# A 180-degree rotation on one core: the second group's turn in four pieces of 2048 columns instead of six with a split last copy

## The chip, the core and the metric

The kernel runs on one core of one Trainium2 chip. The metric is the device time of one execution in microseconds (us). Before the change it is 121.99 us, the median of three runs (121.90 to 122.02 us).

## What is computed

```python
def setup_inputs():
    batch, c, h, w = 32, 3, 256, 256
    return {"x": np.random.randn(batch, c, h, w).astype(np.float32)}

def reference(x):
    return np.rot90(x, k=2, axes=(-2, -1)).astype(np.float32)
```

Each of the 32 x 3 = 96 images of 256 x 256 float32 values is turned by 180 degrees. Seen as one row of 65,536 values, an image is simply reversed. Input and output are 25.17 MB each.

## The kernel before

The 96 rows are cut into three groups of 32 rows. A row of a group is cut into four quarters of E = 16,384 values, and each quarter lies on a partition of its own, so that a group fills a tile of 128 partitions x 64 KiB. The tiles are A, Bt and Ct for groups 0, 1 and 2. All three fit in on-chip memory at the same time, and a tile is turned in place.

To reverse a row one has to reverse the order of its quarters and reverse each quarter in itself. The order of the quarters is handled by a transfer with a reversed index: for A and Ct by the store (`o4[g][:, ::-1, :]`, line 57), for Bt by the load (line 71). The reversal within a quarter is done by the vector engine.

`turn(t, pieces, parts)` (line 75) walks over the first half of the 16,384 columns in `pieces` steps, and for each calls `swap` (line 59), which exchanges a block of w columns at the left with its mirror block at the right. A swap is three copies through the scratch tile T (128 x 2048): the right block reversed into T, the left block reversed into the right one, T into the left one. If `parts` is over 1, the third copy of the last swap of a turn is cut into that many copies. All copies are recorded in the helper `copy` (line 49), in the order of the program.

All transfers are issued from the sync engine's queue (SP), in this order: load A (line 54), load Bt (line 71), load Ct in two parts of 15,872 and 512 columns (lines 72 and 73), store Bt (line 83), store A (line 57), store Ct (line 57). The queue issues the store of Bt when the last copy of Bt's turn is done; the store of A comes behind it in the queue. The vector engine turns A, then Bt, then Ct. Every turn needs its whole load, and every store its whole turn. The profile puts the copies on line 49, whatever the tile, so the tile's name tells the groups apart.

Of the kernel before, what the change touches and what calls it, by code (L numbers as in the profile page):

```python
# [2 lines left out]

os.environ.setdefault("NEURON_RT_ULTRASERVER_MODE", "4")

# [4 lines left out]


@with_exitstack
def kernel(
    ctx: ExitStack,
    tc: tile.TileContext,
    x: bass.AP,
    out: bass.AP,
):
    nc = tc.nc  # L20
    P = 128

    B, C, H, W = x.shape
    L = H * W
    G = 32
    E = L // 4
    J = E // 8

    x4 = x.rearrange("b c h w -> (b c) (h w)").rearrange(
        "(g n) (s e) -> g (n s) e", n=G, s=4)  # L30
    o4 = out.rearrange("b c h w -> (b c) (h w)").rearrange(
        "(g n) (s e) -> g n s e", n=G, s=4)

    xr = x.rearrange("b c h w -> (b c) (h w)").rearrange(
        "(g n) (s e) -> g n s e", n=G, s=4)
    of = out.rearrange("b c h w -> (b c) (h w)").rearrange(
        "(g n) (s e) -> g (n s) e", n=G, s=4)

    pool = ctx.enter_context(tc.tile_pool(name="slots", bufs=1))
    A = pool.tile([P, E], x.dtype, tag="A")  # L40
    Bt = pool.tile([P, E], x.dtype, tag="B")
    Ct = pool.tile([P, E], x.dtype, tag="C")
    T = pool.tile([P, J], x.dtype, tag="T")

    def back(t, lo, hi):
        return t[:, hi - 1:(lo - 1 if lo else None):-1]

    def copy(dst, src):
        c = nc.vector.tensor_copy(out=dst, in_=src)  # L49
        tc.keep_in_program_order(c)  # L50
        return c

    def load(t, g):
        return nc.sync.dma_start(out=t[:, :], in_=x4[g])  # L54

    def store(t, g):
        return nc.sync.dma_start(out=o4[g][:, ::-1, :], in_=t[:, :])

    def swap(t, lo, w, parts=1):
        hi = E - lo - w  # L60
        copy(T[:, 0:w], back(t, hi, hi + w))
        copy(t[:, hi:hi + w], back(t, lo, lo + w))
        step = -(-w // parts)
        for a in range(0, w, step):
            b = min(w, a + step)
            copy(t[:, lo + a:lo + b], T[:, a:b])

    half = E // 2

    load(A, 0)  # L70
    nc.sync.dma_start(out=Bt[:, :], in_=xr[1][:, ::-1, :])
    nc.sync.dma_start(out=Ct[:, 0:E - 512], in_=x4[2][:, 0:E - 512])
    nc.sync.dma_start(out=Ct[:, E - 512:E], in_=x4[2][:, E - 512:E])

    def turn(t, pieces, parts=1):
        step = -(-half // pieces)
        for lo in range(0, half, step):
            w = min(step, half - lo)
            swap(t, lo, w, parts if lo + w == half else 1)

    turn(A, 4)
    turn(Bt, 6, 2)
    nc.sync.dma_start(out=of[1], in_=Bt[:, :])
    store(A, 0)
    turn(Ct, 4)
    store(Ct, 2)


# [1 line left out]
_INS = ['x']  # L90
_OUTS = [((32, 3, 256, 256), 'float32')]


# [23 lines left out]
```

## Time and profile before

One profiled execution took 121.83 us; its span, from the first instruction to the last, is 120.0 us.

| | |
|---|---|
| median of three runs | 121.99 us |
| profiled execution, time / span | 121.83 / 120.0 us |
| vector engine (DVE) busy | 45.2 us, 43 copies |
| data moved | 25.17 MB read, 25.17 MB written |
| load A landed, turn of A starts | 22.5 us |
| load Bt landed, turn of Bt starts | 41.9 us |
| store of Bt issued | 58.28 us |
| store of A issued | 58.67 us |
| turn of Ct starts | 61.43 us |
| store of Ct issued | 76.55 us |

DVE is the vector engine; SPq is the queue instruction with which the sync engine issues a transfer. "COPY T<-A 128x2048" is a copy from tile A to tile T, of 128 partitions by 2048 columns. The share beside a DMA queue is the time that its packets took, as a share of the span of 16 DMA engines. In a view of a stretch of time, a packet is booked in the slice in which it starts; a packet of these transfers is a whole partition's row (64 KiB) and lasts over 2 us. "Us to landing" is the time from the issue of a transfer to the arrival of its last data.

### The profile page before, as it was taken

The page shows a single profiled execution, that of the slowest core. Times are in us where ns is not written, and L with a number is a line of the kernel's source. Part 1 is how long each engine was busy: PE and PEld are TensorE (multiplying, and loading weights), DVE is VectorE, ACT ScalarE, POOL GpSimd, SP SyncE. Part 2 cuts the span into 40 slices and gives each one's busy share as a digit, 9 for nine tenths or more (in the row PEclk, how much of TensorE's full clock was granted, in tenths as well). Part 3 has the DMA queues.
Part 4 walks back from the last instruction along what each step waited for, and adds up shares of the span by engine and source line. Part 5 has one row for each costly group of instructions (what it writes and reads, how often), then busy time and mean ns, then how long its engine had stood idle before and what let it go on. Part 6 is the DMA issues. An engine that isn't in the chain of part 4 may idle for free.

```text
span 120.0 us, 99 instructions
## 1 busy us (share of the span) xinstructions
DVE 45.2 (38%) x43; POOL 0.2 (0%) x4
## 2 busy tenths in 40 slices
DVE  0000000499995099999359999400000000000000
POOL 0000000000000000000000000000000000000000
DMA  9888988898889878977899889988898889888990
GB/s 349 349 349 371 677 349 349 349 699 349 349 349 677 360 338 360 656 338 338 350 534 590 349 349 415 633 349 349 371 677 349 349 349 699 349 349 349 655 393 0
DMA packets 1008, 50.33 MB, mean 419 GB/s; under 512 B 112, under 2 KB 112, under 8 KB 240
## 3 DMA queue, kind: packets, MB, share of 16 engines
q1 hardware_dynamic: 1008, 50.33, 97.4%
HBM read 25.17 MB, written 25.17 MB: 419 GB/s over the span
## 4 chain that ended last, share of the span: by engine, by line
DMA 34%; DVE 26%; another core or an unknown queue 3%; issue 1%; SPq 0%; DVEq 0%
DMA Bt<-in_x_dram 34%; DVE Bt L49 9%; DVE T L49 9%; DVE Ct L49 8%; SPq L54 0%; DVEq L49 0%
## 5 line engine op out<-in xcount | busy, mean ns | idle before, releaser
L49 DVE COPY T<-A 128x2048 f32<-128x2048 f32 x4 | 4.9, 1226 | 22.6 <-DMA A<-in_x_dram 22.5
L49 DVE COPY T<-Bt 128x1366 f32<-128x1366 f32 (+1 forms) x6 | 5.2, 873 | 4.5 <-DMA Bt<-in_x_dram 4.3
L49 DVE COPY T<-Ct 128x2048 f32<-128x2048 f32 x4 | 4.9, 1227 | 3.3 <-DMA Ct<-in_x_dram 3.2
L49 DVE COPY Bt<-T 128x1366 f32<-128x1366 f32 (+1 forms) x7 | 5.3, 770 | 0.2
L49 DVE COPY Bt<-Bt 128x1366 f32<-128x1366 f32 (+1 forms) x6 | 5.2, 872 | 0.2
L49 DVE COPY A<-T 128x2048 f32<-128x2048 f32 x4 | 4.9, 1228 | 0.1
L49 DVE COPY Ct<-Ct 128x2048 f32<-128x2048 f32 x4 | 4.9, 1227 | 0.1
L49 DVE COPY A<-A 128x2048 f32<-128x2048 f32 x4 | 4.9, 1227 | 0.1
L49 DVE COPY Ct<-T 128x2048 f32<-128x2048 f32 x4 | 4.9, 1226 | 0.1
L101 POOL MEMSET const-bfloat16-1.0<- 128x1 bf16 x1 | 0.1, 102 | 0.0
L101 POOL MEMSET const-uint8-127<- 128x1 uint8 x1 | 0.1, 102 | 0.0
L101 POOL MEMSET const-float32-1.0<- 128x1 f32 x1 | 0.1, 99 | 0.0
L101 POOL MEMSET const-float32-0.0<- 128x1 f32 x1 | 0.1, 98 | 0.2 <-issue 0.2
## 6 DMA issues: line engine op xcount, KB each, us to landing
Ct<-in_x_dram SPq DMA_DIRECT2D x1, 7936.0 KB, 58.7
Ct<-in_x_dram SPq DMA_DIRECT2D x1, 256.0 KB, 58.8
A<-in_x_dram SPq DMA_DIRECT2D x1, 21.7
Bt<-in_x_dram SPq DMA_DIRECT2D x1, 40.6
out_dram<-Bt SPq DMA_DIRECT2D x1, 22.4
out_dram<-A SPq DMA_DIRECT2D x1, 41.3
out_dram<-Ct SPq DMA_DIRECT2D x1, 42.7
```

Source lines behind the costliest of these rows:

```text
L49: c = nc.vector.tensor_copy(out=dst, in_=src)
L101: nc = _bacc.Bacc("TRN2", target_bir_lowering=False, num_devices=1)
```

## The change

```diff
     turn(A, 4)
-    turn(Bt, 6, 2)
+    turn(Bt, 4)
     nc.sync.dma_start(out=of[1], in_=Bt[:, :])
     store(A, 0)
     turn(Ct, 4)
```

Before, the step of Bt's turn is ceil(8192 / 6) = 1366 columns: five swaps of 1366 and one of 1362, and the third copy of the last swap is cut into two copies of 681 columns, 19 copies in all. After, the step is 2048 columns: four swaps of three copies, 12 in all, the same as for A and Ct. T, with 2048 columns, is then filled whole by each swap. Nothing else differs; the transfers and their order in the queue are the same.

## The prediction

> **What bounds the kernel now.** I read the page's totals and its one DMA queue first, then the issues with their times to landing, then the timeline around the group that is changed, last the chain of waits, to see whether it agrees.
>
> ```profile
> span 120.0 us, 99 instructions
> DVE 45.2 (38%) x43; POOL 0.2 (0%) x4
> q1 hardware_dynamic: 1008, 50.33, 97.4%
> HBM read 25.17 MB, written 25.17 MB: 419 GB/s over the span
> ```
>
> The vector engine works for 38% of the span; the one queue, q1, keeps the 16 DMA engines occupied for 97.4% of it. Of 120.0 us that leaves 2.6% = 3.1 us in which an average DMA engine is not moving data, and the packet records say where they lie: the first packet starts at 1.74 us, and the last ends at 118.91 us, 1.13 us before the span's end. Those two pieces alone are 2.9 us. So there is next to nothing idle in the middle, where the change is.
>
> The issues (queue instruction, time from issue to landing) locate the joints:
>
> ```profile
> Ct<-in_x_dram SPq DMA_DIRECT2D x1, 256.0 KB, 58.8
> out_dram<-Bt SPq DMA_DIRECT2D x1, 22.4
> out_dram<-A SPq DMA_DIRECT2D x1, 41.3
> out_dram<-Ct SPq DMA_DIRECT2D x1, 42.7
> ```
>
> With the issue starts from the timeline (2.49, 58.28, 58.67 and 76.55 us), these land at 61.3, 80.7, 100.0 and 119.25 us. The steps are 19.4, 19.3 and 19.3 us. Every store moves 8.39 MB, so a step of 19.3 us is 435 GB/s, against 419 over the whole span. The first store, the one the change releases earlier, already lands one full-rate step behind the last load; by the landing events themselves 80.65 - 61.30 = 19.35 us, against 19.30 for the two steps after it. At most 0.05 us can be won at this joint.
>
> The stretch from 56 to 64 us alone, which holds the end of the loads, both issues and the start of the store, says the same:
>
> ```profile
> DMA packets 208, 3.38 MB, mean 422 GB/s; under 512 B 32, under 2 KB 32, under 8 KB 160
> q1 hardware_dynamic: 208, 3.38, 99.0%
> ```
>
> A packet is booked where it starts, so what is counted is the packets that began in these 8 us; by the records they run from 57.34-57.82 us (one value per engine) to 65.3-65.8 us, 7.95 us, of which 99.0% of 8 us = 7.92 us is packet time. No gap over 0.03 us is left on an average engine.
>
> The timeline of the vector engine and of the sync queue:
>
> ```profile
> 22.50 1.23 DVE L49 COPY T<-A 128x2048 f32<-128x2048 f32 x1 [22.50 <-DMA A<-in_x_dram]
> ...
> 36.37 1.23 DVE L49 COPY A<-T 128x2048 f32<-128x2048 f32 x1
> 41.90 0.87 DVE L49 COPY T<-Bt 128x1366 f32<-128x1366 f32 x1 [4.30 <-DMA Bt<-in_x_dram]
> ...
> 57.31 0.94 DVE L49 COPY Bt<-T 128x681 f32<-128x681 f32 x2
> 58.28 0.35 SPq L83 DMA_DIRECT2D out_dram<-Bt  x1
> 58.67 0.61 SPq L57 DMA_DIRECT2D out_dram<-A  x1
> 61.43 1.23 DVE L49 COPY T<-Ct 128x2048 f32<-128x2048 f32 x1 [3.18 <-DMA Ct<-in_x_dram]
> ```
>
> The reader should see two things. The turn of Bt ends at 58.25 us and the store follows at once, so the store is indeed released by that last copy. And the third load lands only at 61.30 us (the Ct turn starts at 61.43): when the store is issued, the DMA engines still have about 2 us of load in front of it.
>
> Last, the chain of waits, which seems to say the opposite:
>
> ```profile
> DMA 34%; DVE 26%; another core or an unknown queue 3%; issue 1%; SPq 0%; DVEq 0%
> DMA Bt<-in_x_dram 34%; DVE Bt L49 9%; DVE T L49 9%; DVE Ct L49 8%; SPq L54 0%; DVEq L49 0%
> ```
>
> The Bt turn stands in it because the chain joins an instruction to the one before it on its engine. It ends with the last Ct copy at 76.53 us, and its shares add up to only 64% of the span, so it never reaches the stores that end the program. I do not take it as the bound.
>
> **The change part by part.**
>
> Copies. Removed: 19 copies for Bt, 17 at 0.87 us and two halves that together take 0.94 us; from 41.90 to 58.25 us, 16.35 us with the gaps between them. Added: 12 copies of 128x2048. The same 12 on A are in the timeline: from 22.50 to 36.37 + 1.23 = 37.60 us, 15.10 us (12 x 1.227 = 14.72 us busy and 11 gaps of 0.034 us); on Ct 61.43 to 76.53 us, again 15.10 us. Same engine, form and scratch tile, so 15.10 us is the price on Bt. The turn is 16.35 - 15.10 = 1.25 us shorter and ends at 57.00 us. The first load of Bt's data into T waits for the landing at 41.80 us as before.
>
> Issues. On the sync queue the store of Bt moves from 58.28 to about 57.03 us, and the store of A behind it from 58.67 to 57.42 us, done by 58.04 us. Behind these the queue waits for the Ct load and then the Ct turn (issue at 76.55 us); neither moves. The vector engine's idle time before the Ct turn grows from 3.18 to about 4.4 us.
>
> DMA engines. This is the path that sets the end, and it gets the same descriptors in the same order. Engine by engine the last load packet ends at 60.45-60.95 us by the packet records, and the first store packet starts within 0.01 us of it. What hides the edit is the tail of the Ct load, from 57.0 to 60.5 us. How much cover is there? The nearest row for the time from issue to first packet is the program's first load: issue at 0.73, first packet at 1.74 us, 1.0 us. The store must so be issued by 60.45 - 1.0 = 59.4 us; before it has 1.2 us to spare, after 2.4 us. If that cover were gone, each us of later release would be one us of the end. A's store is needed at about 80 us, Ct's at about 99 us; both have over 20 us.
>
> Unknown cost. No row shows two store issues at 57.0-58.0 us beside the seventh and eighth of Ct's packets. From below: the joint has 0.05 us to give. From above: the only stretch in which the queue was filled and data moved at a reduced rate is the program's start, where each engine's first packet took 2.64 to 3.36 us against 2.42 us later, so 0.2 to 0.9 us, mean about 0.6 us, with four issues running and the engines starting from idle. The nearest row lies much closer: in this same run the last large Ct packets took 2.342 to 2.359 us while both stores were issued, against 2.342 to 2.347 us for those just before them, 0.01 us more on average. I take 0, since that 0.01 us is paid before and after alike, and keep -0.05 and +0.6 for the range.
>
> Sum: the profiled execution took 121.83 us, of which 120.04 is span and 1.79 lies around it; 121.83 + 0 = 121.83 us. The median of the runs shown is 0.16 us higher, 121.99 us, with 121.90 to 122.02 between them. The forecast for the median is 121.98 us.
>
> **The rivals.**
>
> Faster: the chain is right, and the release of the store sets the end. Then the 1.25 us of the shorter turn come off whole: 120.74 us. For it: line 83 waits for the last Bt copy (16.4 us in the queue's waits), and the chain passes through Bt. Against it: the 19.35 us step of the landings leaves 0.05 us. 4%.
>
> Slower: the earlier stores disturb the end of the Ct load, by running packets among it or by the filling of the queue. The place is 57.0 to 60.5 us; it decides from the first delay on, because three stores follow the load without a gap and every delay of the load's last packet is passed on in full. At the price of the program's start, 0.6 us, this gives 122.6 us. For it: descriptors are now added while a further large packet has still to start, which before was not so. Against it: a rise of 0.01 us when it was tried at 58.28 us, and all transfers land in the order of issue. The Trainium skill's page "DMA: Bandwidth & Descriptors", section "Queues, rings and completion order", says that descriptors of one ring are consumed in ring order on each engine; by that rule a store can't take a turn before the load and this case costs 0, and the order of the landings here agrees. 5%.
>
> The change does not do what it says: wide copies on Bt are slower than on A and Ct, and the store goes out no earlier, or later. Up to 1.2 us later this stays without effect, so the time is that of no change, 121.98 us; it is a part of the forecast's chance (1%).
>
> **How the numbers follow.** About 0.2%, 0.24 us, is what a measurement of this kernel can tell from no change. No change within it: 91%. Faster by more: 4%, all from the first rival. Slower by more: 5%, all from the second. The range is the forecast's own, with the 0.05 us at the joint, the runs' spread of 0.1 us, and on the upper side part of the disturbance: 121.75 to 122.25 us.
>
> **What would show it.** Right: Bt copies of 1.227 us; the turn 15.1 us long; line 83 issued at 57.0 us and its wait for Bt 15.1 us; the time from issue to landing up by 1.25 us for the stores of Bt (23.6) and A (42.5) and unchanged for Ct (42.7); landings still at 61.3, 80.7, 100.0 and 119.25 us. The idle time before Ct's first copy at 4.4 us shows where the 1.25 us went. Wrong: a step from the last load's landing to the first store's other than 19.35 us; a Ct landing later than 61.4 us (second rival); or an end that moves with line 83's issue (first rival).

## The result, and the profile after

The changed kernel takes 122.98 us (median of four runs, 122.92 to 123.02 us), the kernel before 122.00 us (four runs). The ratio is 1.0077, with a 95% interval of 1.006 to 1.0095: about 1.0 us slower. The forecast was no change, 121.98 us, with a range up to 122.25 us.

The page of the changed kernel, its span and the row of the DMA queue (packets, MB, share of 16 engines' span):

```profile
span 121.1 us, 92 instructions
q1 hardware_dynamic: 1008, 50.33, 97.2%
HBM read 25.17 MB, written 25.17 MB: 415 GB/s over the span
```

The share of the queue is as high as before, of a span that is 1.1 us longer: 97.2% of 121.1 us are 117.7 us of packet time, where before 97.4% of 120.0 us were 116.9 us, for the same packets and bytes. So 0.9 of the 1.1 us are not idle time between packets. They lie inside packets that took longer, and only the rate shows it (415 against 419 GB/s).

The timeline of the changed kernel around the group that was changed:

```profile
56.09 1.23 DVE L49 COPY Bt<-T 128x2048 f32<-128x2048 f32 x1
57.34 0.35 SPq L83 DMA_DIRECT2D out_dram<-Bt  x1
57.73 0.61 SPq L57 DMA_DIRECT2D out_dram<-A  x1
62.52 1.23 DVE L49 COPY T<-Ct 128x2048 f32<-128x2048 f32 x1 [5.21 <-DMA Ct<-in_x_dram]
```

The turn of Bt was as short as forecast: 42.21 to 57.32 us, 15.1 us. It started 0.3 us later than before because one of the 16 DMA engines was 0.3 us behind since the first load (last landing of A at 22.79 in place of 22.47 us; averaged over the engines 22.32 and 22.28 us). So line 83 was issued 0.94 us earlier than before, not 1.25. But the Ct turn starts at 62.52 us in place of 61.43: the load in front of the store became slower. The issues, with their time to landing:

```profile
Ct<-in_x_dram SPq DMA_DIRECT2D x1, 256.0 KB, 59.9
out_dram<-Bt SPq DMA_DIRECT2D x1, 24.4
out_dram<-A SPq DMA_DIRECT2D x1, 43.3
out_dram<-Ct SPq DMA_DIRECT2D x1, 42.7
```

With the issue starts (2.47, 57.34, 57.73 and 77.65 us) the landings are at 62.4, 81.7, 101.0 and 120.35 us. The steps are 19.3 us each, as before; the last load alone is 1.1 us later, and everything behind it moves along. The stretch from 56 to 64 us, as in the prediction:

```profile
DMA packets 199, 2.79 MB, mean 348 GB/s; under 512 B 32, under 2 KB 32, under 8 KB 160
q1 hardware_dynamic: 199, 2.79, 93.0%
```

Before, 3.38 MB began in these 8 us, now 2.79 MB. Part of that is the edge of the window, since a row of 64 KiB counts where it starts. By the packet records the cause is narrow: each engine's last large packet of the Ct load (62 KB, started at 57.46 to 58.13 us) took 2.59 to 3.81 us, mean 3.25, where before it took 2.34 to 2.36. The large packet of each engine before it took 2.34 us, and the store's own packets (64 KB) 2.42 us, as before the change.

### The profile page after: what moved, and what is told of

Read it like the earlier page. It is cut to its first block, busy times and chain, and to the rows that moved or that the text cites. A ratio compares the mean times of both kernels' runs of the same rounds, so it can differ in the third digit from the quotient of the medians.

```text
span 121.1 us, 92 instructions
## 1 busy us (share of the span) xinstructions
DVE 44.2 (36%) x36; POOL 0.2 (0%) x4
## 3 DMA queue, kind: packets, MB, share of 16 engines
q1 hardware_dynamic: 1008, 50.33, 97.2%
## 4 chain that ended last, share of the span: by engine, by line
DMA 34%; DVE 25%; another core or an unknown queue 4%; issue 1%; SPq 0%; DVEq 0%
DMA Bt<-in_x_dram 34%; DVE T L49 8%; DVE Ct L49 8%; DVE Bt L49 8%; SPq L54 0%; DVEq L49 0%
## 5 line engine op out<-in xcount | busy, mean ns | idle before, releaser
L49 DVE COPY T<-Bt 128x2048 f32<-128x2048 f32 x4 | 4.9, 1227 | 4.4 <-DMA Bt<-in_x_dram 4.3
L49 DVE COPY Bt<-T 128x2048 f32<-128x2048 f32 x4 | 4.9, 1227 | 0.1
L49 DVE COPY Bt<-Bt 128x2048 f32<-128x2048 f32 x4 | 4.9, 1227 | 0.1
## 6 DMA issues: line engine op xcount, KB each, us to landing
out_dram<-Bt SPq DMA_DIRECT2D x1, 24.4
out_dram<-A SPq DMA_DIRECT2D x1, 43.3
out_dram<-Ct SPq DMA_DIRECT2D x1, 42.7
```

## The experiments

Two numbers are given for a run: its median (the kernel before, run beside it, had 121.98 to 122.02 us), and the mean duration of those last large Ct packets ("last packets"), which is read from the one profiled execution. The "joint" is the step from the landing of the Bt load to the landing of the Bt store, each averaged over the 16 engines: 38.79 us before, 39.65 after, so 0.86 us lost there. Edits are shown against the changed kernel, lines left out are marked with "..."; repeated copies write the same values once more.

**e1: the wide copies kept, the store held back.**

```diff
     turn(Bt, 4)
+    copy(Bt[:, half - 2048:half], T[:, 0:2048])
     nc.sync.dma_start(out=of[1], in_=Bt[:, :])
```

> The changed kernel with one copy of 2048 columns done twice at the end of Bt's turn: the wide copies stay, and the store of Bt is issued about 1.26 us later, near 58.3 us, where the kernel before issued it. Theory 1 (a large load packet that starts while or just after stores are issued is slowed; before, no large packet started after 58.28 us): the last Ct packets take about 2.35 us again, and the time is 122.0 us, as before. Theory 2 (a store queued while a whole large load packet has still to start disturbs the loads, however long before): also 122.0 us. Rival 3 (the wide copies on Bt themselves, or the smaller number of instructions, cost the 1.0 us): 123.0 us or more, and last Ct packets of 2.6 to 3.8 us.

121.99 us, ratio 0.999 (0.9979 to 1.0001). The queue's issue and its time to landing in this run:

```profile
58.87 0.35 SPq L84 DMA_DIRECT2D out_dram<-Bt  x1
out_dram<-Bt SPq DMA_DIRECT2D x1, 22.2
```

Last packets 2.35 us, joint 38.76 us. The loss is gone although no copy became narrower: rival 3 falls, and the issue time is what matters.

**e2: held back by less.**

```diff
     turn(Bt, 4)
+    copy(Bt[:, half - 640:half], T[:, 2048 - 640:2048])
```

> As the run with the 2048-column copy, but the repeated copy has 640 columns, so the store of Bt is issued about 0.5 us later than in the changed kernel, at 57.5 to 57.8 us, while some engines have just started their last large Ct packet and others are about to. Theories 1 and 2: only the engines that start this packet after the issue are slowed, so the extra time lies between 0 and 1 us, and within the run long packets are those with late starts: 122.0 to 122.8 us. Rival 3: 123.0 us.

122.36 us, ratio 1.0031 (1.0015 to 1.0046), store issued at 57.69 us. Eight of the 16 last packets were slowed (2.54 to 3.26 us). They are mostly the early starters, 57.55 to 57.75 us, and five of them were already running when the issue came; of the seven started at 57.83 us and later six were clean. So "a packet that starts beside an issue" is not the rule. The size of the loss between none and all fits both theories.

**e3: the store issued earlier still.**

```diff
-    turn(Bt, 4)
+    for lo in range(0, half, 2048):
+        if lo + 2048 < half:
+            swap(Bt, lo, 2048)
+        else:
+            copy(T[:, 0:2048], back(Bt, half, half + 2048))
+            copy(Bt[:, half:half + 2048], back(Bt, lo, lo + 2048))
```

> The changed kernel without the last copy of Bt's turn (columns 6144 to 8191 of group 1 stay unturned): the store of Bt is issued 1.26 us earlier, near 55.8 to 56.1 us, and the store of A is through by about 57.0 us. Large Ct packets start at 55.0 to 55.5 and at 57.3 to 57.8 us, so none starts while the stores are issued. Theory 1, if the disturbance lasts only as long as the queue instructions: no packet over 2.4 us, 122.0 us. Theory 1 with a lag of up to 1 us after the issue: part of the last packets slowed, 122.3 to 123.0 us. Theory 2: at least as slow as the changed kernel, 123.0 us or more.

122.97 us, ratio 1.0078 (1.0049 to 1.0108). Issued at 55.95 us, both queue instructions done at 56.95 us, before any last packet started (57.44 us). The large packets that were running during the issue took 2.34 to 2.36 us, and the last ones 2.72 to 3.84 us, mean 3.16. Theory 1 in its first form falls; theory 2 is left.

**e4: the store of A held back.**

```diff
     nc.sync.dma_start(out=of[1], in_=Bt[:, :])
-    store(A, 0)
-    turn(Ct, 4)
+    swap(Ct, 0, 2048)
+    copy(T[:, 0:64], A[:, 0:64])
+    copy(A[:, 0:64], T[:, 0:64])
+    store(A, 0)
+    for lo in range(2048, half, 2048):
+        swap(Ct, lo, 2048)
     store(Ct, 2)
```

> The changed kernel with the store of Bt issued at the same place, but the store of A held back by two 64-column copies on A behind the first swap of Ct, to about 66 us, long before its data are due at 81 us. If the number of transfers queued sets the price, about half of it goes: 122.3 to 122.6 us. If the first issue alone does the harm (theory 1 or 2 with the store of Bt as the cause), nothing changes: 122.9 to 123.0 us. If the store of A does it, since its issue runs at 57.7 to 58.3 us, after the last packets' start, 122.0 us.

123.04 us, ratio 1.0085 (1.0055 to 1.0114); store of Bt at 57.18, store of A at 66.91 us; last packets 3.12 us, joint 39.71 us. The one store of Bt is enough.

**e5: the store queued 11 us ahead.**

```diff
-    turn(Bt, 4)
+    swap(Bt, 0, 2048)
+    swap(Bt, 2048, 2048)
```

> The changed kernel with only the first two of the four swaps of Bt's turn (columns 4096 to 12287 of group 1 stay unturned): the store of Bt is issued near 49.5 us, over 11 us before the loads end. Theory 2a (a store that is known to the DMA engines while they still load costs a fixed price at the joint of about 1 us): 122.9 to 123.1 us, slow packets only among the last large Ct packets and the 512-column tail, those of 50 to 55 us start at 2.35 us each. Theory 2b (the price grows with the time that the store is queued): well over 123.1 us, long packets from 50 us on. Theory 1 (only packets that start beside an issue are slowed): about 122.0 us or a few slowed packets near 50 us.

123.02 us, ratio 1.009 (1.0061 to 1.012).

```profile
49.69 0.35 SPq L84 DMA_DIRECT2D out_dram<-Bt  x1
Ct<-in_x_dram SPq DMA_DIRECT2D x1, 256.0 KB, 59.9
out_dram<-Bt SPq DMA_DIRECT2D x1, 32.2
```

The store lands at 81.9 us, as in the changed kernel, where it was issued 7.6 us later. The large packets that started from 50 to 57 us took 2.34 to 2.37 us; only the last large one (mean 3.49 us) and a few of the tail's were slowed. The price is nearly fixed (the median as in the changed kernel, the joint, 39.96 us, 0.3 us more), and it is paid at the end of the load. Theory 2a holds against 2b.

**e6: too late.**

```diff
     turn(Bt, 4)
+    copy(Bt[:, half - 2048:half], T[:, 0:2048])
+    copy(Bt[:, half - 2048:half], T[:, 0:2048])
+    copy(Bt[:, half - 2048:half], T[:, 0:2048])
```

> The changed kernel with three repeated copies of 2048 columns: the store of Bt is issued near 60.9 us, later than the 59.4 us that the prediction worked out as the latest. All theories: no slowed load packet, tail clean; but the DMA engines run dry, first store packet near 61.9 us in place of 60.5 to 61.0, so the time is 1.0 to 1.4 us over that of the kernel before: 123.0 to 123.4 us. It shows the other edge of the window.

123.08 us, ratio 1.0096 (1.0067 to 1.0125). Issued at 60.95 us, first store packets at 61.79 to 61.94 us: 0.84 to 0.99 us from issue to first packet, as the prediction read from the first load (1.0 us). Last packets 2.34 us. Each engine was idle for 0.4 to 0.9 us between the load and the store, and the queue's share of the span shows it, 96.9%:

```profile
q1 hardware_dynamic: 1008, 50.33, 96.9%
```

The idle time would have been longer, but for some Ct packets from 43 to 56 us that took up to 2.61 us in this execution, 0.4 us per engine in all, though no store was queued. Why is not known. The store's first packet is set by its own issue here, so this does not change the end.

**e8: a load joins the queue in place of the store.** The tail of the Ct load is taken from the start of the program to here:

```diff
-    nc.sync.dma_start(out=Ct[:, E - 512:E], in_=x4[2][:, E - 512:E])
...
-    turn(Bt, 4)
+    for lo in (0, 2048, 4096):
+        swap(Bt, lo, 2048)
+    copy(T[:, 0:2048], back(Bt, half, half + 2048))
+    copy(Bt[:, half:half + 2048], back(Bt, 6144, half))
+    copy(Ct[:, E - 512:E], T[:, 0:512])
+    nc.sync.dma_start(out=Ct[:, E - 512:E], in_=x4[2][:, E - 512:E])
+    copy(Bt[:, 6144:half], T[:, 0:2048])
+    copy(Bt[:, 6144:half], T[:, 0:2048])
     nc.sync.dma_start(out=of[1], in_=Bt[:, :])
```

> The 512-column tail of the Ct load is not issued at the start but held back by a 512-column copy into it, until about 56.3 us; the store of Bt follows at 58.8 to 59.1 us, behind a repeated copy. So a load, in place of a store, joins the queue while large Ct packets have still to end. If any transfer that joins the queue there disturbs the load (the issue itself, its descriptors): packets of 2.6 to 3.8 us and about 123.0 us. If only a store behind a load does: packets of 2.35 us and 122.0 us (up to 122.2 if the tail's packets show a gap).

121.93 us, ratio 0.9992 (0.9975 to 1.0008).

```profile
56.20 0.33 SPq L86 DMA_DIRECT2D Ct<-in_x_dram  x1
58.59 0.35 SPq L89 DMA_DIRECT2D out_dram<-Bt  x1
```

Last packets 2.36 us, joint 38.76 us. Neither the issue nor its descriptors do the harm; a load queued at 56.20 us costs nothing, a store at 55.95 us cost all (e3). This load is small, 16 KB per engine; a store of that size is tried below (e15). For a load of full size the kernel before shows the same: the loads of Bt and Ct are queued from 1.16 us on, and the last packets of the loads of A and Bt in front of them took 2.42 us. Nor does a store slow a store: Bt's last store packets, with the store of A behind them, took 2.42 us.

**e9 and e10: how far ahead the store reaches.** Both with the two swaps of e5; e9 loads Ct in one piece, e10 with a longer tail:

```diff
-    nc.sync.dma_start(out=Ct[:, 0:E - 512], in_=x4[2][:, 0:E - 512])
-    nc.sync.dma_start(out=Ct[:, E - 512:E], in_=x4[2][:, E - 512:E])
+    load(Ct, 2)                                                       # e9
...
+    nc.sync.dma_start(out=Ct[:, 0:E - 4096], in_=x4[2][:, 0:E - 4096])   # e10
+    nc.sync.dma_start(out=Ct[:, E - 4096:E], in_=x4[2][:, E - 4096:E])
```

> The early issue of 49.5 us (only two of Bt's four swaps, columns 4096 to 12287 of group 1 unturned), and the Ct load in one transfer of 64 KB rows without the 512-column tail. It asks how far ahead of the load's end the store takes effect. If the reach is a number of descriptors, ten or more (the tail's eight and two for completion counts stood between the slowed packet and the store), then with large packets alone all Ct packets after about 51 us are slowed, and the time is well over 123.1 us. If the reach is a stretch of bytes or of time before the load's end, only the last 64 KB packet (start 57.5 to 58 us) is slowed, by about 1 us: 122.9 to 123.1 us.

> The early issue of 49.5 us again (same columns unturned), with a Ct load of 12,288 and 4096 columns: the last 4.8 us of the load run in 16 KB packets of 0.6 us each. Reach in descriptors (ten or more): the last 48 KB packet, which ends near 55.6 us, is slowed, and the 16 KB packets too: over 123.1 us. Reach in bytes or time: the 16 KB packets before about 57.5 us run at 0.61 us each, and only the last three to six of each engine are slowed, together by about 1 us: 122.9 to 123.1 us.

e9: 123.05 us, ratio 1.0085 (1.0068 to 1.0103). All Ct packets up to the last but one took 2.42 to 2.44 us (64 KB each), and the last, started at 58.00 to 58.63 us, 3.23 to 3.81 us. e10: 123.00 us, ratio 1.0081 (1.0064 to 1.0099). Of each engine's eight 16 KB packets the first four took 0.61 us. Of the last four, started from 58 us on, two or three took longer, up to 1.25 us, mostly the second and third of them; the very last took 0.61 us again on most engines. So the reach is counted in bytes (or time), not in descriptors: the slowing falls within about the last 64 KB that each engine loads, some 2.4 us at full rate.

**e7, e13, e14: small transfers, first try.** The swaps of Bt in another order, so that columns 0 to 2047 are written last, and a small transfer ahead of the large store: e7 a store of 512 columns, e13 a transfer of them into an on-chip tile S, e14 meant as the control of e7 (both stores behind the repeated copies). The edit of e7:

```diff
-    turn(Bt, 4)
-    nc.sync.dma_start(out=of[1], in_=Bt[:, :])
+    for lo in (2048, 4096, 6144, 0):
+        swap(Bt, lo, 2048)
+    nc.sync.dma_start(out=of[1][:, 0:512], in_=Bt[:, 0:512])
+    copy(Bt[:, 512:2048], T[:, 512:2048])
+    copy(Bt[:, 1448:2048], T[:, 1448:2048])
+    nc.sync.dma_start(out=of[1][:, 512:E], in_=Bt[:, 512:E])
```

> Bt's swaps in the order 2048, 4096, 6144, 0, so that columns 0 to 2047 are written last. A store of 512 columns of Bt (2 KB rows, 16 KB per DMA engine) goes out at 57.0 to 57.4 us, the other 15,872 columns after two repeated copies, at 58.5 to 58.9 us. Theory 2 with a price that is set by the bytes that can be read ahead: at most the time of 16 KB, 0.6 us, of slowing, so 122.1 to 122.6 us. Theory 2 with a fixed price for any early store: about 1 us, 123.0 us. No price for so small a store: 122.1 us (the 2 KB packets cost 0.08 us more than their share of large ones).

> As the run with the small early store (512 columns of Bt, at 57.0 to 57.4 us), but this transfer goes to an on-chip tile in place of HBM, and all of Bt is stored at 58.5 to 58.9 us. It adds 16 KB for each DMA engine, eight packets of 0.084 us, 0.67 us. If the price comes from reading on-chip memory ahead while the load still writes there: about 0.9 us more, 123.5 to 123.7 us, last large Ct packets over 2.5 us. If it comes from a write to HBM being queued behind reads from it: none, 122.6 to 122.8 us, large packets of 2.35 us.

> The run with the small early store again, with both stores of Bt (512 and 15,872 columns) issued after the two repeated copies, near 58.5 to 59.3 us. If the early issue is what that run paid for: no slowed packet, 122.0 to 122.2 us. If the small transfer itself, its 2 KB rows or the order of the swaps costs the 0.9 us: 122.9 us.

e7: 122.88 us, ratio 1.0079 (1.005 to 1.0109); last packets 2.67 us. e13: 123.00 us, ratio 1.0076 (1.0056 to 1.0095); 2.64 us. e14: 122.82 us, ratio 1.0061 (1.0043 to 1.0079); 2.89 us. None of them decides. The large store at 58.6 to 58.9 us may have cost something too, behind the small transfer, but that is not shown: the last packets of e7 took as long as those of e15 below, where the large store came later. Of the loss of e7 the joint, averaged over the engines, shows only 0.35 us; most of the rest lies with one engine that was late from the first load on (22.90 us). e14 was no control, since the small store waits only for the copies that write its own columns and went out at 57.29 us, as in e7.

**e15, e16, e17: the same with the large store at 59.5 us or later.** In e15 and e16 three repeated copies stand between the small transfer and the large store; in e17 two of them stand ahead of the small store, the second rewriting columns 0 to 1023. The swaps are those of e7.

```diff
+    nc.sync.dma_start(out=of[1][:, 0:512], in_=Bt[:, 0:512])      # e15
...
+    nc.sync.dma_start(out=S[:, :], in_=Bt[:, 0:512])              # e16
...
+    copy(Bt[:, 512:2048], T[:, 512:2048])
+    copy(Bt[:, 512:1536], T[:, 512:1536])
+    copy(Bt[:, 1024:2048], T[:, 1024:2048])
+    nc.sync.dma_start(out=of[1][:, 512:E], in_=Bt[:, 512:E])      # e15
...
```

> A store of 512 columns of Bt near 57.3 us (16 KB for each DMA engine), the other 15,872 columns by three repeated copies only near 59.6 us. Only the small store is early. If the price is set by the bytes of the early store (16 KB, 0.6 us at full rate): 122.3 to 122.7 us. If any store queued there costs all of it: 122.9 to 123.1 us. If the price of e7 came from the large store: 122.0 to 122.2 us.

> As e15, but the small early transfer goes from Bt to an on-chip tile, and all of Bt is stored near 59.6 us; eight more packets of 0.084 us, 0.67 us, so 122.67 us without any price. If reading on-chip memory ahead does the harm, the price is that of e15, on top of 122.67 us, and the large Ct packets are slowed as there. If the write to HBM does it: 122.6 to 122.8 us and large packets of 2.35 us.

> The control: the 512 columns are written again at the end, so that their store goes out near 58.9 us, the rest near 59.6 us. No store early: no slowed packet, 122.0 to 122.2 us. If it takes the time of e15, the small transfer itself is what costs, not when it is issued.

The small transfers in e15, e16 and e17, in this order, and the large store of e17:

```profile
57.09 0.35 SPq L84 DMA_DIRECT2D out_dram<-Bt  x1
```

```profile
57.49 0.53 SPq L85 DMA_DIRECT2D S<-Bt  x1
```

```profile
58.95 0.35 SPq L86 DMA_DIRECT2D out_dram<-Bt  x1
59.55 0.34 SPq L88 DMA_DIRECT2D out_dram<-Bt  x1
```

e17: 121.99 us, ratio 0.9998 (0.9989 to 1.0007), last packets 2.35 us: a small store of its own costs nothing when it is late. e15: 122.39 us, ratio 1.0031 (1.0021 to 1.0042), last packets 2.66 us: issued 1.9 us earlier, the same store costs 0.4 us, about two thirds of the time of its own 16 KB per engine (0.6 us). In the profiled execution, the slowest of ten, the last packets lost 0.3 us; another 0.4 us went into Ct packets from 43 to 56 us, before any store was queued, as in e6. e16: 123.03 us, ratio 1.0075 (1.0051 to 1.0098), last packets 2.60 us. Of its 1.05 us, 0.67 us are the packets it adds, so about 0.4 us are left, as in e15, though its small transfer writes no HBM. By the joint its loss is smaller: 39.62 - 0.67 = 38.95 us, 0.2 us over before; in this run one engine was again late from the first load on (22.93 us). A write to HBM is not needed for the slowing; that both prices are the same is not shown.

**e11: the start of the program.** The kernel of e1, with the later loads held back (the edit against e1):

```diff
     load(A, 0)
+    tc.keep_in_program_order(nc.vector.memset(Bt[:, 0:4096], 0.0))
     nc.sync.dma_start(out=Bt[:, :], in_=xr[1][:, ::-1, :])
```

> The kernel with the 2048-column copy repeated (store of Bt issued near 58.3 to 58.9 us), and the loads of Bt and Ct held back to about 5 us by a vector memset of 4096 columns of Bt. It asks whether the slow first packets of A (2.6 to 3.6 us) come from the issues behind them. If the issues or their descriptors slow them: first packets near 2.42 us, end 0.4 to 0.6 us earlier, 121.4 to 121.6 us. If it is the start itself (cold engines): 122.0 us, first packets as before, and A's second and third packets at 2.42 us although the issues now run beside them.

122.03 us, ratio 1.0003 (0.9994 to 1.0013). The loads of Bt and Ct were issued at 5.15 to 6.9 us, and A's first packets still took 2.51 to 3.36 us; the second ones, beside the issues, took 2.42 to 2.46 us. The slow start is not the work of the issues behind it. So it was no row for a price of issues either. The run also shows that the edge is not sharp: the store of Bt, issued at 58.47 us, found 13 of the 16 last packets clean, but three took 2.45 to 2.63 us.

**e12: the store released by the load.** The Ct load cut at 13,824 columns in place of 15,872, a tile S of 64 columns, and behind the short turn

```diff
     turn(Bt, 4)
+    copy(S[:, 0:64], Ct[:, 0:64])
+    copy(Bt[:, half - 64:half], T[:, 2048 - 64:2048])
```

> The changed kernel with the short turn, but the store of Bt is released by the load: the Ct load is cut at 13,824 columns, and two 64-column copies behind Bt's turn wait for the landing of that first part (near 58.3 us), so the store is issued near 58.8 us whatever the turn's length. If the price hangs on when the store is queued relative to the load's end, it goes: no packet slowed, tail clean, 121.9 to 122.0 us. If the short turn or the wide copies matter in any other way: 122.9 us.

Issued at 58.83 us:

```profile
58.83 0.35 SPq L86 DMA_DIRECT2D out_dram<-Bt  x1
out_dram<-Bt SPq DMA_DIRECT2D x1, 22.2
```

122.19 us, ratio 1.0016 (1.0006 to 1.0025). The joint is 38.84 us: 0.8 us of the loss are back with the short turn. The other 0.2 us are not at the joint; in the profiled execution one engine is 0.3 us late from the first load on (22.80 us), and the first store packets take 2.42 to 2.47 us. Why is not known. It beats neither the kernel before nor e1.

## Why the prediction was wrong

By its own steps:

- **The bound, and no idle time to win at the joint: right.** No run was faster than before beyond its interval, and the steps between the stores stayed at 19.3 us.
- **Copies and issues: right in the main.** 15.1 us for the turn; a wait of line 83 for Bt of 15.2 us (15.1 forecast). The issue came at 57.34 us (57.03 forecast), since that load of Bt landed 0.3 us later. The store of Bt took 24.4 us to land (23.6), that of A 43.3 (42.5), that of Ct 42.7 (42.7); the first two are off by the delay of the load.
- **The latest issue, 59.4 us: in line with the runs.** e6 gives 0.84 to 0.99 us from issue to first packet, so 59.5 to 59.6 us; no run had its only store of Bt issued there.
- **"What hides the edit is the tail of the Ct load", more cover is harmless: wrong.** There are two edges. The prediction worked out the late one and took time ahead of it for spare. The early one lies between 57.7 and about 58.5 us, just where the kernel before stood (58.28 us):

| store of Bt issued, us | run | last large packets, mean us | median, us |
|---|---|---|---|
| 49.69 | e5 | 3.49 | 123.02 |
| 55.95 | e3 | 3.16 | 122.97 |
| 57.18 | e4 | 3.12 | 123.04 |
| 57.34 | changed kernel | 3.25 | 122.98 |
| 57.69 | e2 | 2.61 | 122.36 |
| 58.28 | before | 2.35 | 122.00 |
| 58.47 | e11 | 2.39 | 122.03 |
| 58.59 | e8 | 2.36 | 121.93 |
| 58.87 | e1 | 2.35 | 121.99 |
| 60.95 | e6 | 2.34 | 123.08 |

- **The term that failed is "Unknown cost": "I take 0".** It measured 0.9 us at the joint and 1.0 us in all. The row it rested on, the packets beside the issue at 58.28 us, lay on the harmless side of the edge, and was carried over to an issue 1 us earlier. The reason given for it ("that 0.01 us is paid before and after alike") assumed that the price has no step. Its bound from above, +0.6 us, was too low as well.
- **The rival that came true is "slower", in its place but not in its mechanism.** 57.0 to 60.5 us is where it happened, and the delay was passed on in full, as it said. But it is neither the filling of the queue (a load queued there costs nothing, e8; the number of stores doesn't matter, e4) nor a store that takes turns throughout (packets before the last 64 KB are untouched, e5). Nor is the condition that it named, a large packet still to start, the edge: in e2 five of the slowed packets had started before the issue. Its price of 0.6 us came from the program's start, which e11 shows to be another matter.
- **The ring order was read for more than it says.** The rule of the Trainium skill ("DMA: Bandwidth & Descriptors", section "Queues, rings and completion order") held as far as it goes: the landings kept the order of issue in every run. It says nothing of what a queued transfer costs the one ahead of it, and 0 was concluded from it. The same page of the Trainium skill, section "Two DMAs through the same engine are not ordered", says that descriptors are pipelined, with separate queues for an engine's read and write sides.

What the runs support: a transfer that reads on-chip memory, queued behind a load 3 us or more before the load's end, slows that load within the last 64 KB of each engine. How long before is an estimate: the undisturbed load would end 3.0 us after the start of an engine's last large packet (2.34 us and eight tail packets of 0.084 us), which puts the issue 2.4 us before that end, averaged over the engines, in the kernel before (no packet slowed), 3.1 us in e2 (eight of 16) and 3.4 us in the changed kernel (all). The loss depends on the bytes that are queued there: 0.4 us for 16 KB per engine (e15), about 1 us for a whole store; no size between was run. That the engine's read side runs ahead into the store and takes time from the load's writes fits this, and the sentence of the Trainium skill. It was only argued: no run shows the read side by itself, and why the data read ahead do not shorten the store afterwards stays open.

## What to carry to other kernels

Where loads hand over to stores on busy DMA engines, look for a window for the release of the first store. Here issues from 58.3 to 58.9 us cost almost nothing, about 1.9 to 2.4 us before the load's end, and on either side of them the runs lost up to 1 us (57.3 us and earlier, and 60.95 us). A row that shows an operation to be free at one time is a bound for that time only; before an issue is moved, ask what is in flight at the new place, and price the move from below and above with the uncertain end in the chances. And a queue that is busy for 97% of the span can still be slower: compare the packets' durations and the rate, not the share.

## What was not expected of the hardware

- A store queued early slows the load in front of it: 2.35 to 3.25 us for the last 62 KB packet of each engine (after), while a load queued at such a time does not (2.36 us, e8).
- Once the store is early enough, the price hardly grows with the time in the queue: 0.86 us at the joint when issued at 57.34 us, 0.90 us at 55.95 us (e3), 1.17 us at 49.69 us (e5) and 0.93 us at 49.70 us (e10), with medians of 122.97 to 123.02 us.
- The first packets of this program take longer than the 2.42 us of later ones, whether other transfers are issued beside them (2.64 to 3.36 us, before) or not (2.51 to 3.36 us, e11).
